# The first pair of b in two transfers of four rows (8 KB packets) in place of one of eight rows (16 KB packets)

## Chip, cores, metric

One core of one Trainium2 chip. The metric is the device time of one execution in microseconds. The profile's span, from the first to the last instruction, is some 1.8 us shorter than that time.

## The reference

```python
batch, m, k, n = 16, 512, 512, 512
a: (batch, k, m) float32      b: (batch, n, k) float32
out = np.matmul(a.transpose(0, 2, 1), b.transpose(0, 2, 1)).astype(np.float32)
```

The product sums over k. a lies with k first and is used as it comes; b lies with n first, and this kernel turns it on the chip. 33.6 MB are read and 16.8 MB written.

## The kernel before

Two batches of b form a pair. One transfer loads a pair into one of three buffers. VectorE casts it to bf16 in two halves, PE turns it, VectorE copies it out of PSUM. The SyncE queue (SP in the profile) issues all loads and the last stores; the ScalarE queue issues the other stores.

```python
b_v = b.rearrange("(p g) (ni r) k -> p (g ni) r k", g=2, r=NR)   # NR = 8 rows of 2 KB: 16 KB a partition
LOADS = 4; PAIRS = 3; OUTS = 5; LAG = 3; TAIL = 3
...
def run_sp(sp):
    for i in range(B):
        for p in ([0] if i == 0 else [(i + 1) // 2] if i % 2 and i + 1 < B else []):
            if p >= PAIRS:
                sp.wait_ge(turned, p - PAIRS + 1)
            sp.dma_start(b_sb[p % PAIRS][:], b_v[p]).then_inc(b_in[p % PAIRS], 16)
        s, use = i % LOADS, i // LOADS
        if use:
            sp.wait_ge(summed, MO * (i - LOADS) + 1)
        ...
        sp.dma_start(a_sb[s][:], a_v[i]).then_inc(a_in[s], 16)
...
def cast_b(p, h):                      # on VectorE, h = 0 and 1
    n = 3 if h and p + 1 == H else 1
    r = slice(h * NR // 2, (h + 1) * NR // 2)
    dve.wait_ge(b_in[p % PAIRS], 16 * (p // PAIRS + 1))
    dve.tensor_copy(b_bf[:, r, :], b_sb[p % PAIRS][:, r, :]).then_inc(bc_go, n)
```

Of the kernel before, what the change touches and what calls it, by code (L numbers as in the profile page):

```python
# [11 lines left out]
def kernel(  # L12
# [13 lines left out]
    NR = 2 * N // P  # L26
# [9 lines left out]
    b_v = b.rearrange("(p g) (ni r) k -> p (g ni) r k", g=2, r=NR)  # L36
# [3 lines left out]
    PAIRS = 3  # L40
# [10 lines left out]
    with tc.tile_critical():  # L51
# [4 lines left out]
        b_sb = [sb(f"b_sb{s}", [P, NR, K], f32) for s in range(PAIRS)]  # L56
# [12 lines left out]
        b_in = [sem(f"b_in{s}") for s in range(PAIRS)]  # L69
# [13 lines left out]
        def store(eng, j, part=slice(0, 2)):  # L83


            eng.dma_start(
                out_v[2 * j + part.start:2 * j + part.stop].rearrange("b p mo n -> p b mo n"),
                o_sb[j % OUTS][:, part],
            ).then_inc(o_out[j % OUTS] if j + OUTS < H else stored, 16)

        def run_sp(sp):
            for i in range(B):

                for p in ([0] if i == 0 else [(i + 1) // 2] if i % 2 and i + 1 < B else []):
                    if p >= PAIRS:
                        sp.wait_ge(turned, p - PAIRS + 1)
                    sp.dma_start(b_sb[p % PAIRS][:], b_v[p]).then_inc(b_in[p % PAIRS], 16)
                s, use = i % LOADS, i // LOADS
                if use:
                    sp.wait_ge(summed, MO * (i - LOADS) + 1)  # L100
                if i % 2 == 0 and i // 2 >= OUTS:

                    sp.wait_ge(o_out[i // 2 % OUTS], 16 * (i // 2 // OUTS))
                sp.dma_start(a_sb[s][:], a_v[i]).then_inc(a_in[s], 16)

            for j in range(H - TAIL, H - 1):
                sp.wait_ge(summed, MO * (2 * j + 2) + 3)
                store(sp, j)

            sp.wait_ge(summed, MO * (B - 1) + 1)  # L110
            sp.wait_ge(half_go, 1)
            store(sp, H - 1, slice(0, 1))
            sp.wait_ge(last_go, 3)
            store(sp, H - 1, slice(1, 2))
            sp.reg_mov(all_stored, 16 * STORED)
# [21 lines left out]
        def copy_out(eng, i, rm, go):  # L137

            q = rm if isinstance(rm, int) else rm.stop - 1
            eng.wait_ge(summed, MO * i + q + 1)  # L140
            copy = eng.copy if eng is nc.scalar else eng.tensor_copy
            h = q // 2
            p = rm - 2 * h if isinstance(rm, int) else slice(None)
            copy(o_sb[i // 2 % OUTS][:, i % 2, rm, :], o_ps[h][:, p, :]).then_inc(go, 1)  # L144

        def run_dve(dve):
            def cast_b(p, h):

                n = 3 if h and p + 1 == H else 1
                r = slice(h * NR // 2, (h + 1) * NR // 2)  # L150
                dve.wait_ge(b_in[p % PAIRS], 16 * (p // PAIRS + 1))
                dve.tensor_copy(b_bf[:, r, :], b_sb[p % PAIRS][:, r, :]).then_inc(bc_go, n)  # L152

            def turn(p, g):




                if g == 0:
                    dve.wait_ge(turned, p + 1)  # L160
                dve.tensor_copy(  # L161
                    bt_sb[g][:].rearrange("p j (ni r) -> p j ni r", r=NR),
                    bt_ps[:].rearrange("p j r (g ni) -> p g j ni r", g=2)[:, g],
                ).then_inc(bt_go, 1)

            cast_b(0, 0)
            cast_b(0, 1)
            turn(0, 0)
            for p in range(H):
                if p + 1 < H:  # L170
                    cast_b(p + 1, 0)
                copy_out(dve, 2 * p, slice(0, 2), od_go)
                turn(p, 1)
                if p + 1 < H:
                    cast_b(p + 1, 1)
                    copy_out(dve, 2 * p + 1, slice(0, 2), od_go)
                    turn(p + 1, 0)
            copy_out(dve, B - 1, slice(0, 2), last_go)
# [13 lines left out]
        def run_pe(pe):  # L192
# [41 lines left out]
            with pe.Fori(0, H) as _i:  # L234
# [6 lines left out]
                half(1, 1)  # L241

        run_sp(nc.sync)
        run_pool(nc.gpsimd)
        run_dve(nc.vector)
# [35 lines left out]
```

## Time and profile before

| | before |
|---|---|
| time, median of 6 runs | 124.83 us (124.61 to 125.09) |
| span of the profiled run | 123.0 us |
| PE / VectorE / ScalarE busy | 70% / 46% / 38% |
| 16 DMA engines busy, of the span | 97.3% (77.2 + 20.1) |
| packets, bytes | 5648, 50.33 MB, 409 GB/s over the span |

The last two rows decide how this kernel is read. The DMA engines are the busy ones, and they are busy from their first packet to their last (100.1% of the stretch from 1.9 to 121.5 us), so the time is made of a start, a block of packets and an end. The rows of the page that show it stand in the prediction.

### The profile page before, as it was taken

Reading aid. Unit: us, or ns where it says so; the run is one execution under the profiler, and the core shown is the slowest. Engines: PE = TensorE matmul, PEld = TensorE weight load, DVE = VectorE, ACT = ScalarE, POOL = GpSimd, SP = SyncE. Lnnn points to the kernel's source line nnn. Section 1 sums busy time; section 2 is a strip of 40 time slices with the busy share of each in tenths; the row PEclk is TensorE's granted clock in tenths of the full one; section 3 lists DMA queues with packets and bytes.
Section 4 is the critical chain, followed back from the end, with each engine's and each line's share of the span. In section 5 each row is a group of like instructions: output and inputs, shape, how many; then the busy total and the mean of one; then the engine's idle time right before and its main releaser. Section 6 shows DMA issues by size and latency. Waiting matters only on the chain. (4 is left out here: it accounts for less than half of the span.)

```text
span 123.0 us, 1086 instructions
## 1 busy us (share of the span) xinstructions
PE 86.1 (70%) x400; PEld 49.7 (40%) x400; DVE 56.4 (46%) x48; ACT 46.8 (38%) x34; POOL 0.7 (1%) x6
## 2 busy tenths in 40 slices
PE   0006497997999799779930799965992679979600
PEld 0006344642755464346410546442640526437300
DVE  0016368478295755917039107780719306171200
ACT  4003209537717903176300950329230490750300
POOL 2000000000000000000000000000000000000000
PEclk9999999999999999999995557999999558999995
DMA  4999999999999999999999999999999999999992
GB/s 91 394 400 458 400 424 456 429 394 456 426 397 448 434 376 432 426 440 440 416 421 429 458 408 418 429 426 437 453 397 432 426 426 426 429 426 426 429 424 115
DMA packets 5648, 50.33 MB, mean 409 GB/s; under 512 B 528, under 2 KB 528, under 8 KB 528
## 3 DMA queue, kind: packets, MB, share of 16 engines
q1 hardware_dynamic: 4288, 39.85, 77.2%
q10 hardware_dynamic: 1360, 10.49, 20.1%
HBM read 33.55 MB, written 16.78 MB: 409 GB/s over the span
## 5 line engine op out<-in xcount | busy, mean ns | idle before, releaser
L219 PE MATMUL o_ps<-bt_sb,a_bf 128*128 128x512 bf16 x256 | 65.1, 403 | 7.1 <-PEq L194 6.6
L135 ACT CAST a_bf<-a_sb 128x2048 bf16<-128x2048 f32 x16 | 30.4, 1900 | 40.8 <-DMA a_sb<-in_a_dram 40.8
L219 PEld LDWEIGHTS o_ps<-bt_sb,a_bf 128*128 128x128 bf16 x256 | 28.5, 115 | 37.5 <-issue 15.0
L205 PE MATMUL bt_ps<-identity,b_bf 128*128 128x128 f32 x144 | 24.3, 323 | 22.7 <-PEq L194 22.7
L144 DVE COPY o_sb<-o_ps 128x1024 f32<-128x1024 f32 x16 | 19.6, 1224 | 35.8 <-PE o_ps L219 35.8
L205 PEld LDWEIGHTS bt_ps<-identity,b_bf 128*128 128x128 f32 x144 | 22.2, 212 | 28.2 <-issue 27.2
L152 DVE CAST b_bf<-b_sb 128x2048 bf16<-128x2048 f32 x16 | 19.5, 1221 | 19.1 <-DMA b_sb<-in_b_dram 19.1
L144 ACT COPY o_sb<-o_ps 128x1024 f32<-128x1024 f32 (+1 forms) x17 | 16.4, 962 | 28.0 <-PE o_ps L219 28.0
L161 DVE COPY bt_sb<-bt_ps 128x1024 f32<-128x1024 f32 x16 | 19.5, 1216 | 3.1 <-PE bt_ps L205 3.1
L135 ACT ACT_TABLE_LOAD x1 | 1.3, 1283 | 0.9 <-SPq L51 0.9
L122 POOL TENSOR_SCALAR_AFFINE_SELECT identity<-identity 128x128 f32<-128x128 f32 x1 | 0.3, 294 | 0.2 <-POOL identity L120 0.2
L120 POOL MEMSET identity<- 128x128 f32 x1 | 0.2, 205 | 0.7 <-SPq L51 0.7
L265 POOL MEMSET const-bfloat16-1.0<- 128x1 bf16 x1 | 0.1, 102 | 0.0
L265 POOL MEMSET const-uint8-127<- 128x1 uint8 x1 | 0.1, 102 | 0.0
L265 POOL MEMSET const-float32-0.0<- 128x1 f32 x1 | 0.1, 99 | 0.2 <-issue 0.2
L265 POOL MEMSET const-float32-1.0<- 128x1 f32 x1 | 0.1, 99 | 0.0
## 6 DMA issues: line engine op xcount, KB each, us to landing
b_sb<-in_b_dram SPq DMA_DIRECT2D x8, 2048.0 KB, 20.4
a_sb<-in_a_dram SPq DMA_DIRECT2D x16, 1024.0 KB, 17.5
out_dram<-o_sb ACTq DMA_DIRECT2D x5, 2048.0 KB, 15.2
out_dram<-o_sb SPq DMA_DIRECT2D x2, 2048.0 KB, 13.6
out_dram<-o_sb SPq DMA_DIRECT2D x2, 1024.0 KB, 6.3
```

Source lines behind the costliest of these rows:

```text
L120: pool.memset(identity[:], 0.0).then_inc(id_go, 1)
L122: pool.affine_select(out=identity[:], in_=identity[:], compare_op=mybir.AluOpType.not_equal, fill=1.0, base=0, pattern=[[-1, P]], channel_ ...
L135: act.copy(a_bf[i % 2][:], a_sb[s][:]).then_inc(ac_go, 1)
L144: copy(o_sb[i // 2 % OUTS][:, i % 2, rm, :], o_ps[h][:, p, :]).then_inc(go, 1)
L152: dve.tensor_copy(b_bf[:, r, :], b_sb[p % PAIRS][:, r, :]).then_inc(bc_go, n)
L161: dve.tensor_copy(bt_sb[g][:].rearrange("p j (ni r) -> p j ni r", r=NR), bt_ps[:].rearrange("p j r (g ni) -> p g j ni r", g=2)[:, g],).the ...
L205: last = pe.transpose(bt_ps[:, j, r, :], w[:, r, j, :], identity[:])
L219: last = pe.matmul(o_ps[h][:, q, :], a_r[:, rk, 2 * h + q, :], bt_h[:, rk // 2, rk % 2, :], start=(rk == 0), stop=(rk == KO - 1),)
L265: nc = _bacc.Bacc("TRN2", target_bir_lowering=False, num_devices=1)
```

## The change

Its look is that of a split for an early start: load half of the first pair, cast it while the other half comes. But the wait that would use it is not there: both casts of pair 0 wait for both halves. What is left is a smaller packet and a second transfer, for the first pair alone.

```diff
-                    sp.dma_start(b_sb[p % PAIRS][:], b_v[p]).then_inc(b_in[p % PAIRS], 16)
+
+                    for r in (slice(0, NR // 2), slice(NR // 2, NR)) if p == 0 else (slice(0, NR),):
+                        sp.dma_start(
+                            b_sb[p % PAIRS][:, r, :], b_v[p][:, r, :]
+                        ).then_inc(b_in[p % PAIRS], 16)
...
-                dve.wait_ge(b_in[p % PAIRS], 16 * (p // PAIRS + 1))
+                dve.wait_ge(b_in[p % PAIRS], 16 * (p // PAIRS + 1 + (p % PAIRS == 0)))
```

## The prediction

> **What bounds the kernel now.** I first read the table of the page that cuts the span into 40 slices, because it says at once whether any engine is full from beginning to end.
>
> ```profile
> PE   0006497997999799779930799965992679979600
> DVE  0016368478295755917039107780719306171200
> ACT  4003209537717903176300950329230490750300
> ...
> DMA  4999999999999999999999999999999999999992
> GB/s 91 394 400 458 400 424 456 429 394 456 426 397 448 434 376 432 426 440 440 416 421 429 458 408 418 429 426 437 453 397 432 426 426 426 429 426 426 429 424 115
> ```
>
> No compute engine is full; the DMA row reads 9 in all slices but the first and the last. So the 16 DMA engines never run dry, and the span (123.0 us) is a start, a solid block of transfers, and an end. The page's chain of work that ended last holds 5% of the span in PE and stops at 110 us, so it does not describe the body. To measure the block I asked the DMA view for the stretch from 1.9 to 121.5 us alone:
>
> ```profile
> DMA packets 5648, 50.33 MB, mean 421 GB/s; under 512 B 528, under 2 KB 528, under 8 KB 528
> q1 hardware_dynamic: 4288, 39.85, 79.4%
> q10 hardware_dynamic: 1360, 10.49, 20.7%
> ```
>
> The shares are busy time over 16 engines: 79.4 + 20.7 = 100.1% of 119.6 us. Every packet of the program lies in it and there is no gap. The packet records of the trace have the first data packet at 1.956 us and the last one ending at 121.45 us, and the sum of all packet times after the start divided by 16 is 119.76 us (slightly above the 119.49 us between them, since one packet's end overlaps the next one's start). Hence span = 1.96 (start) + 119.5 (packets) + 1.5 (end of the last packet to the end of the program), and the metric is 1.8 us above the span (124.81 against 123.0). Only three things can move it: when the first packet starts, how long the packets take in total, and whether something opens a gap.
>
> Is the end also set by transfers? The timeline of the last stretch shows compute ending early:
>
> ```profile
> 115.02 0.59 ACT L144 COPY o_sb<-o_ps 128x512 f32<-128x512 f32 x1 [4.74 <-PE o_ps L219]
> 115.93 0.59 ACT L144 COPY o_sb<-o_ps 128x512 f32<-128x512 f32 x1 [0.32 <-PE o_ps L219]
> ```
>
> The last store is issued at 116.54 us and lands at 121.93 us. It is 1 MB, which is 2.47 us of packets (8 an engine at 309 ns), so they began near 119.0 us, behind stores still queued. Some 1.5 us of compute slack remains even at the end. At the start, the timeline has
>
> ```profile
> 0.95 0.39 SPq L97 DMA_DIRECT2D b_sb<-in_b_dram  x1
> ...
> 8.81 2.36 DVE L152 CAST b_bf<-b_sb 128x2048 bf16<-128x2048 f32 x2 [8.81 <-DMA b_sb<-in_b_dram]
> ```
>
> Issue at 0.95, first packet 1.0 us later, first use at 8.81, when the last of the 16 engines has reported (8.79 us in the records). While the compute engines wait for this, the DMA engines already move a0.
>
> [...] the median 16 KB packet takes 611 ns, 16384 / 611 = 26.8 GB/s an engine, 429 GB/s on 16. [...] the median 8 KB packet takes 309 ns, so two take 618 ns against 611 ns for one of 16 KB, 7 ns for one more packet. [...] each of the new halves is exactly 1 MiB over 128 partitions, and the a loads of this case are such transfers already. [...]
>
> **The change, part by part.**
>
> *Packets.* Pair 0 of b is 2 MB: now 128 packets of 16 KB, 8 an engine. Afterwards 256 of 8 KB, 16 an engine. Cost: 16 x 309 - 8 x 611 = 4944 - 4888 = +56 ns an engine. All engines are full, so this lies wholly on the path.
>
> *Completion.* One more transfer means 16 more semaphore packets, one an engine, 9 ns each in the records: +9 ns on the path. The 5648 packets become 5648 + 128 + 16 = 5792.
>
> *Issue.* One more issue on the SP queue, which takes 0.39 to 0.47 us with its gap to the next. The first half is issued at 0.95 us as before, so the first packet does not move. Everything behind it is issued some 0.45 us later, but finds a queue with microseconds of work: by the time a0 is issued (1.39, then about 1.85 us) no packet has moved at all, and a0's first packets follow some 5 us of b0. The last of the seven opening loads (a3) goes out at 4.23 us and lands at 28.5 us. The next refill waits on summed until 16.66 us, far later. Cost 0.
>
> *Waits.* The kernel's text decides this, not the transfer: for slot 0 both casts wait for one count of 16 more, that is 32 for pair 0, and both halves must have landed before either cast. So no cast starts on the first half early. The first cast starts when the second half has landed, about 8.81 + 0.065 = 8.87 us. For pairs 3 and 6 the offset only makes up for the extra 16 already counted. The listing of instructions by engine confirms that nothing else moves: PE, DVE, ACT and POOL keep their order, and SP has one transfer more.
>
> *Start-up.* The first packets are slow: 22 packets before 4 us take 0.65 to 1.92 us instead of 0.61; their excess over 611 ns is 12.5 us together, or 0.78 us an engine. If this is a wait that comes once, whatever the packet's size, it stays; if it goes with the bytes of the first packet, half of it could go. I take no change.
>
> Sum: +0.056 + 0.009 = +0.07 us, 124.81 -> 124.88 us, called 124.9.
>
> **The rivals.**
>
> *A quicker start.* Were the 0.78 us of slow first packets tied to their size, 8 KB packets might save up to about half, 0.4 us, giving 124.5. For it: the first packet of an engine is the slow one and is now twice as short. Against it: second packets in the records are slow as well (1.2 us), and then all become 611 ns at about the same moment, 3.5 to 4 us, which looks like a delay in time rather than in bytes. I give it one chance in four.
>
> *Half rows read more slowly.* Each half reads 8 KB, skips 8 KB, and so on, instead of running through memory. [...] Against: the b packets of 16 KB and the a packets of 8 KB already run at practically the same rate (429 and 424 GB/s)[...]. No view shows a read with this skip, so a few per cent of chance stay.
>
> *An earlier cast.* If the first cast could start on the first half, it would come some 2.5 us sooner (8 x 309 ns). The wait excludes it, and even then the compute engines would only wait longer later, since the DMA row has no gap to close. Worth 0.
>
> *A gap in the queue.* The phases of stores and loads might shift. The records show packets slowed to as much as 1.1 us at 42 to 48 us, where stores begin to mix with loads; they add up to 0.17 us an engine. A shift may change that by 0.1 us either way.
>
> **Range and chances.** The three times before run from 124.61 to 125.06, so a median of three may be off by 0.2 us. With 0.1 us for phases and the start-up chance of -0.4 us, 124.5 to 125.3 should hold 8 times in 10. Two per cent is 2.5 us. Nothing that this change touches can give 2.5 us back (the start-up excess is 0.78 us whole), and only the rival of the half rows could cost as much: faster 0.01, same 0.97, slower 0.02.
>
> **What would show it.** The changed profile should have 5792 packets, 50.33 MB, and the DMA row at 9 from slice 2 to 39; 1024 - 128 = 896 packets of 16 KB; 8 KB packets of pair 0 at 309 ns after the first few microseconds; the first cast at 8.8 to 9.0 us, not at 6; the span within 0.4 us of 123.0. A first cast below 8.6 us with fewer slow packets would speak for the quicker start; pair 0's packets well above 309 ns after 4 us for the half rows; a slice below 9 in the middle of the DMA row for a gap. Any of the last two of more than 0.4 us would make the prediction wrong.

The +0.07 us is made of measured packet times (611, 309 and 9 ns).

## More of the kernel before

One more view is needed for what follows: three stretches of the span, with the columns of the engines (busy time and number of instructions for PE, PE's weight loads, VectorE, ScalarE, GpSimd), then PE's clock, the busy share of the DMA engines, and GB/s. This is the kernel before:

```profile
1.00:9.00 8.00, 0.00 (x0) 0.00 (x0) 0.19 (x1) 1.19 (x1) 0.50 (x2) 1.00 0.86 325
40.00:50.00 10.00, 9.05 (x47) 5.30 (x46) 6.45 (x6) 4.11 (x4) 0.00 (x0) 1.00 0.99 413
50.00:100.00 50.00, 35.97 (x160) 20.23 (x159) 23.80 (x21) 20.05 (x15) 0.00 (x0) 0.85 1.01 429
```

The busy share is full in the second row (0.99) although less is moved than in the third (413 against 429 GB/s). A packet that is held up counts as busy in these records: in that row packets of 16 KB took up to 1.13 us in place of their median of 0.611, and no engine was without one. So where packets stalled here, the GB/s show it and the busy share does not. At 40 to 50 us the first store is issued (40.47 us) and its packets start to mix with the loads (from 44.04 us).

## The result, and the profile after

125.21 us, median of 6 runs (124.75 to 125.28), against 124.83 us. The ratio is 1.0023, 95% interval 1.0002 to 1.0043: within 2%, and inside the predicted range. A ratio is the mean time of one kernel's fast runs over that of the other's fast runs in the same rounds, so it is not quite the ratio of the medians.

The page of the changed kernel has the DMA rows and the packet count that the prediction named:

```profile
DMA  3999999999999989999999999999999999999992
GB/s 77 390 430 446 419 425 441 435 406 443 435 401 433 441 329 427 425 446 435 427 412 427 446 422 417 427 427 454 417 422 427 425 427 430 427 425 427 427 425 85
DMA packets 5792, 50.33 MB, mean 408 GB/s; under 512 B 544, under 2 KB 544, under 8 KB 544
```

The count of 5792 is exactly as predicted. The DMA row is not quite: it was to read 9 from slice 2 to slice 39, and the fifteenth slice (43 to 46 us) reads 8, with 329 GB/s where the row of before has 376. The prediction had named such a digit as the sign of a gap. By the packet records there is hardly one: between 6 us and the last 4 us of transfers each engine is without a packet for 0.03 us on the mean. It is slow packets that fill the slice. The timeline of the start, SP's issues and the first cast (columns: start, length, engine, line, operation, tiles, and what ended the idle time before):

```profile
0.95 0.86 SPq L99 DMA_DIRECT2D b_sb<-in_b_dram  x2
1.86 0.42 SPq L108 DMA_DIRECT2D a_sb<-in_a_dram  x1
...
8.67 2.36 DVE L156 CAST b_bf<-b_sb 128x2048 bf16<-128x2048 f32 x2 [8.67 <-DMA b_sb<-in_b_dram]
```

The second issue costs 0.47 us of the queue's time. The first cast comes at 8.67 us, not at 6, and a little before the 8.8 to 9.0 us of the prediction. The three stretches of the changed kernel, to be held against those of before:

```profile
1.00:9.00 8.00, 0.00 (x0) 0.00 (x0) 0.33 (x1) 1.19 (x1) 0.50 (x2) 1.00 0.88 334
40.00:50.00 10.00, 8.99 (x46) 5.29 (x46) 6.54 (x6) 4.00 (x4) 0.00 (x0) 1.00 0.99 402
50.00:100.00 50.00, 35.12 (x154) 19.99 (x156) 23.67 (x21) 19.65 (x14) 0.00 (x0) 0.85 1.01 429
```

At the start the changed kernel is ahead: 9 GB/s over 8 us is 0.07 MB, or 0.17 us at 429 GB/s. At 40 to 50 us it loses 11 GB/s over 10 us, 0.11 MB, 0.26 us. From 50 us on both run at the same rate. So two traces put the small loss at the place where stores begin. Is that the change, or chance?

To compare many traces I used the packet records in one way throughout. The *start excess* is the sum of what the packets up to 10 us took beyond 611 ns (16 KB) or 309 ns (8 KB), divided by 16 engines. The *store stall* is the same sum over the nine microseconds after the issue of the first store. The *engine idle* is the stretch from the first packet's start to the last packet's end, less the mean work of an engine (the sum of all packet times, each less the 3.5 ns by which consecutive packets of an engine overlap in the records, divided by 16). It holds the idle time of both ends of the stream: counted from the packets under way at each moment, the trace before has 0.33 us an engine before 6 us, where the engines begin one after another, and 0.57 us in the last 4 us, where they end one after another.

### The profile page after: what moved, and what is told of

Read it like the earlier page. It is cut to its first block, busy times and chain, and to the rows that moved or that the text cites. A ratio compares the mean times of both kernels' runs of the same rounds, so it can differ in the third digit from the quotient of the medians.

```text
span 123.4 us, 1079 instructions
## 1 busy us (share of the span) xinstructions
PE 85.5 (69%) x392; PEld 49.7 (40%) x400; DVE 56.5 (46%) x48; ACT 46.9 (38%) x34; POOL 0.7 (1%) x6
## 2 busy tenths in 40 slices
DMA packets 5792, 50.33 MB, mean 408 GB/s; under 512 B 544, under 2 KB 544, under 8 KB 544
## 5 line engine op out<-in xcount | busy, mean ns | idle before, releaser
L223 PE MATMUL o_ps<-bt_sb,a_bf 128*128 128x512 bf16 x248 | 63.1, 402 | 8.4 <-PEq L198 7.4
```

What stands on the lines that cost most here:

```text
L223: last = pe.matmul(o_ps[h][:, q, :], a_r[:, rk, 2 * h + q, :], bt_h[:, rk // 2, rk % 2, :], start=(rk == 0), stop=(rk == KO - 1),)
```

## The experiments

Twelve runs, each of five rounds against the kernel before; all results correct.

| run | median us | ratio (95% interval) |
|---|---|---|
| aa_before | 124.90 | 1.0009 (0.9993 to 1.0024) |
| aa_after | 125.17 | 1.0026 (1.0009 to 1.0043) |
| aa_after2 | 125.06 | 1.0017 (1.0000 to 1.0034) |
| split_all | 125.51 | 1.0058 (1.0043 to 1.0073) |
| pad_all | 125.66 | 1.0068 (1.0053 to 1.0084) |
| parts_first | 129.61 | 1.0377 (1.0361 to 1.0394) |
| pad_first | 125.18 | 1.0019 (1.0005 to 1.0032) |
| split_mid | 124.97 | 1.0010 (0.9992 to 1.0028) |
| early_cast | 124.98 | 1.0005 (0.9992 to 1.0018) |
| early_cast_2 | 125.19 | 1.0025 (1.0008 to 1.0041) |
| late_start | 125.76 | 1.0064 (1.0046 to 1.0082) |
| quarter_first | 125.37 | 1.0042 (1.0018 to 1.0066) |

**Is it real? aa_before, aa_after, aa_after2.** No edit: the two kernels again, against the kernel before.

> The kernel before against itself. The change measured +0.3 us (ratio 1.0023, interval 1.0002 to 1.0043). If that is real, this pair must give a ratio within 0.001 of 1. If two runs of one text differ by 0.002 or more, +0.3 us is within what chance gives. Trace: packets slowed at 40 to 50 us (where stores begin) cost 0.19 us an engine in the trace before and 0.49 us in the trace after; theory 'chance' has this number vary from run to run of one kernel, theory 'split' has it at 0.19 again.

> The changed kernel once more. Theory 'accounting plus chance' (7 ns for each further packet and 9 ns for the semaphore packet, +0.07 us in all, the rest of +0.3 us is the size of the stall where stores begin): ratio 1.0005, anything from 0.999 to 1.0025. Theory 'split' (the split start shifts the phase so that the stall is larger every time): ratio 1.002 to 1.003 again, and a stall of about 0.49 us an engine at 40 to 50 us in the trace.

> The changed kernel a third time, beside early_cast_2 on the same chip. 'Real' says 1.002 to 1.003 as twice before, landings spread by 0.8 us before 40 us and a stall over 0.3 us; 'chance' says anything from 0.999 to 1.0025 and a stall that may be as small as 0.1 us.

The kernel before against itself gives 1.0009; the changed kernel 1.0023, 1.0026 and 1.0017, every lower bound at 1.0000 or above. So the change costs something, some 0.2% or 0.27 us, about four times the 0.07 us of the accounting. A single ratio of 1.001 means nothing here, as the control shows. The store stall was 0.07 us in aa_before, 0.32 in aa_after and 0.45 in aa_after2. "Chance", as I had put it, falls for the stall. The landings' spread (how far apart the 16 engines report one load just before 40 us, without the first and the last of them) was 0.53 us in aa_after2 and not 0.8: that half of the expectation missed.

**Eight doses: split_all.**

```diff
-                    for r in (slice(0, NR // 2), slice(NR // 2, NR)) if p == 0 else (slice(0, NR),):
+                    for r in (slice(0, NR // 2), slice(NR // 2, NR)):
-  16 * (p // PAIRS + 1 + (p % PAIRS == 0))
+  32 * (p // PAIRS + 1)
```

> All eight pairs of b in two halves, eight times the dose. Accounting: 8 x (8 x 7 + 9) = 0.52 us, ratio 1.004, 6800 packets (5648 + 8 x 144). If each split costs the 0.3 us that was measured for one: +2.4 us, ratio 1.019. If the +0.3 us comes only from the start, or from chance: 1.004 to 1.006.

+0.72 us (0.0058 x 124.8), 6800 packets. A split pair does not cost 0.27 us each time: eight would be over 2 us. The rest of the chain, seven more split pairs, adds 0.45 us to the one split of the changed kernel, 0.06 us a pair.

**Small packets without a second transfer: pad_all and pad_first.** The two halves of a partition's row get a gap of 64 bytes between them in SBUF, for all pairs or for the first one only.

```diff
-        b_sb = [sb(f"b_sb{s}", [P, NR, K], f32) for s in range(PAIRS)]
+        b_sb = [sb(f"b_sb{s}", [P, 2, NR // 2 * K + 16], f32) for s in range(PAIRS)]
-                    sp.dma_start(b_sb[p % PAIRS][:], b_v[p]).then_inc(b_in[p % PAIRS], 16)
+                    sp.dma_start(b_sb[p % PAIRS][:, :, :NR // 2 * K],
+                                 b_v[p].rearrange("p (h r) k -> p h (r k)", h=2)).then_inc(b_in[p % PAIRS], 16)
...                                   # the casts read the same places; pad_first: the gap for p == 0 only
```

> All eight pairs in one transfer each, but the two halves of a row lie 64 bytes apart in SBUF, so every packet is 8 KB: packet size without a second transfer. Accounting: 8 x 8 x 7 ns = 0.45 us, ratio 1.0036, 5648 + 1024 = 6672 packets, none of 16 KB. If the second issue and landing is what costs, and not the packets: 1.000.

> The first pair in one transfer whose packets are 8 KB (a gap of 64 bytes between the halves of a row in SBUF), the other pairs as before. Accounting: 8 more packets an engine of 3.5 to 7 ns, 0.03 to 0.06 us, ratio 1.0004. If 8 KB packets at the start are what costs +0.3 us: 1.0025, with a larger stall at 40 to 50 us than the 0.07 and 0.18 us an engine of the two traces of the kernel before.

+0.85 us and +0.24 us. This would have been taken for "the packets alone do it", had the timeline not been read. Kernel pad_first:

```profile
0.95 0.65 SPq L104 DMA_DIRECT2D b_sb<-in_b_dram  x1
...
9.35 1.23 DVE L161 CAST b_bf<-b_sb 128x2048 bf16<-128x2048 f32 x1 [9.35 <-DMA b_sb<-in_b_dram]
```

The issue of the transfer with two pieces a partition takes 0.65 us instead of 0.39, and its first packet starts at 2.38 us instead of 1.96. That is a delay of 0.42 us of its own, so these two kernels do not isolate the packet size. What pad_first does tell: its store stall is 0.14 us, as with the kernel before, though pair 0 came in the same 8 KB packets. The page of pad_first counts 5776 packets, the 128 more that this takes. The expectation that 8 KB packets at the start enlarge that stall failed, in one trace and with a later start.

**A second transfer without small packets: parts_first.**

```diff
-                    for r in (slice(0, NR // 2), slice(NR // 2, NR)) if p == 0 else (slice(0, NR),):
+                    for r in (slice(0, P // 2), slice(P // 2, P)) if p == 0 else (slice(0, P),):
-                            b_sb[p % PAIRS][:, r, :], b_v[p][:, r, :]
+                            b_sb[p % PAIRS][r], b_v[p][r]
```

> The first pair in two transfers as in the change, but each of 64 partitions with packets of 16 KB: a second issue and landing without smaller packets. Accounting: one more semaphore packet, under 10 ns, ratio 1.000. If the second transfer at the start is what costs +0.3 us (twice measured, 1.0023 and 1.0026): 1.0025.

+4.7 us, which neither theory had. The DMA view of this kernel, 3.5 to 7.5 us, while pair 0 comes:

```profile
DMA packets 68, 0.85 MB, mean 213 GB/s; under 512 B 16, under 2 KB 16, under 8 KB 16
q1 hardware_dynamic: 68, 0.85, 101.6%
```

All engines busy, half the rate: a 16 KB packet takes 1.28 us (median from 4.3 to 7 us) in place of 0.611. That is 213 GB/s where 16 KB in 0.611 us on each of 16 engines make 429. Why was not shown: no other run changes the partitions of a transfer. As a control this kernel is spoilt. It does show, once more, what a delay at the start is worth: the first cast slips from 8.81 to 13.30 us, by 4.49 us, and the time grows by about as much (4.7 us).

**The same split elsewhere: split_mid.**

```diff
-  if p == 0 else (slice(0, NR),):
+  if p == 4 else (slice(0, NR),):
-  16 * (p // PAIRS + 1 + (p % PAIRS == 0))
+  16 * (p // PAIRS + 1 + (p in (4, 7)))
```

> The split on pair 4 (issued near 55 us) and not on pair 0: the same packets and transfers in number, but the start and the place where stores begin as before. If the change costs by what it does to the start and to the stall at 40 to 50 us: 1.000 to 1.0005, stall 0.07 to 0.18 us. If a split pair costs 0.3 us wherever it stands: 1.0025.

1.0010, no different from the control (1.0009), with the same 5792 packets. The intervals overlap that of the changed kernel, so the time alone does not separate them; the stall does, 0.21 us in the one trace. But the expectation had placed pair 4 wrongly. SP's timeline of split_mid:

```profile
27.60 0.91 SPq L99 DMA_DIRECT2D b_sb<-in_b_dram  x2
```

Pair 4 is issued at 27.60 us, not near 55 (that is pair 6), and its packets pass just where stores begin: all 312 data packets of loads in the nine microseconds after the first store's issue are of 8 KB, where the kernel before has 105 of 16 KB and 103 of 8 KB. So split_mid keeps the start as before, but not that place. It shows that a split pair passing there is not enough for the large stall; it does not show what a split in an undisturbed stretch costs. Split_mid, 40 to 50 us, and below it aa_after2, the changed kernel:

```profile
40.00:50.00 10.00, 8.98 (x47) 5.25 (x46) 6.54 (x6) 4.10 (x4) 0.00 (x0) 1.00 1.01 419
```

```profile
40.00:50.00 10.00, 9.00 (x46) 5.51 (x48) 6.53 (x7) 3.85 (x4) 0.00 (x0) 1.00 1.00 406
```

**The wait that the change left in place: early_cast, early_cast_2.** The first half gets a semaphore of its own, so that its cast need not wait for the second.

```diff
+        b_first = sem("b_first")
-  ).then_inc(b_in[p % PAIRS], 16)
+  ).then_inc(b_first if p == 0 and r.start == 0 else b_in[p % PAIRS], 16)
-  dve.wait_ge(b_in[p % PAIRS], 16 * (p // PAIRS + 1 + (p % PAIRS == 0)))
+  if p == 0 and h == 0:
+      dve.wait_ge(b_first, 16)
+  else:
+      dve.wait_ge(b_in[p % PAIRS], 16 * (p // PAIRS + 1))
```

> The change with a semaphore of its own for the first half, so that the first cast no longer waits for the second half. First cast at 6.2 us (the last engine's landing of the first half in the trace after is 6.17) and not 8.67. If the kernel is bound by its transfers, the time stays that of the changed kernel, ratio 1.0015 to 1.003 against the kernel before. If the wait for both halves was what kept the change from paying, up to 2.4 us come back: 0.981 to 0.99.

> The early first cast again. Its ratio was 1.0005 (0.9992 to 1.0018) where the changed kernel had 1.0023 and 1.0026, though both move the same packets. If the early cast gives something back, it must again be 0.001 to 0.002 below aa_after2; if that was chance, both agree within 0.001.

The timeline of early_cast on VectorE:

```profile
6.18 1.23 DVE L160 CAST b_bf<-b_sb 128x2048 bf16<-128x2048 f32 x1 [6.18 <-DMA b_sb<-in_b_dram]
8.66 1.23 DVE L160 CAST b_bf<-b_sb 128x2048 bf16<-128x2048 f32 x1 [1.26 <-DMA b_sb<-in_b_dram]
```

The cast starts 2.5 us earlier, and the time is 1.0005 and 1.0025, around that of the changed kernel. The difference that the first run seemed to show was gone in the second (1.0025 beside 1.0017). Starting compute earlier bought nothing here, where the transfers have no gap.

**The start itself: late_start.** The kernel before, its first issue held until the identity is built.

```diff
         def run_sp(sp):
+            sp.wait_ge(id_go, 2)
```

> The kernel before, with the first transfer issued only when the identity is ready (last POOL instruction ends at 1.83 us), so near 1.9 us in place of 0.95 us. If span = start + full block of packets + end, the whole 0.9 to 1.0 us shows: ratio 1.0075. If slack anywhere takes it up (compute waiting for b, buffers): nearer 1.000. It also tells how the two padded kernels read, whose first packet came 0.42 us later.

The first packet starts at 2.88 us (1.96 before), 0.92 us later; the time grows by 0.80 us (0.0064 x 124.98; interval 0.57 to 1.02). The start is on the path, nearly or fully one for one. At that rate the 0.42 us of the padded kernels would cost some 0.37 us (an estimate, 0.42 x 0.80 / 0.92). All of pad_first cost 0.24 us (0.06 to 0.40), so how much of its delay reached the time is not settled.

**The change's dose at the start: quarter_first.**

```diff
-  for r in (slice(0, NR // 2), slice(NR // 2, NR)) if p == 0 else (slice(0, NR),):
+  for r in [slice(x, x + 2) for x in range(0, NR, 2)] if p == 0 else [slice(0, NR)]:
-  16 * (p // PAIRS + 1 + (p % PAIRS == 0))
+  16 * (p // PAIRS + 1 + 3 * (p % PAIRS == 0))
```

> The change's own dose: pair 0 in four transfers of two rows, 4 KB packets. Accounting by spacing: 24 more packets an engine and three more semaphore packets, 3.5 and 5.5 ns each, 0.10 us, ratio 1.0008. If smaller packets at the start leave the 16 engines further apart and the stall where stores begin grows with it (spread of a load's landings just before 40 us, without first and last: 0.5 us before, 0.8 us after; stall 0.07 to 0.18 and 0.33 to 0.58 us): 1.0025 or more with stall over 0.3 us.

1.0042, 0.52 us, more than the change itself and five times the accounting. But not through the stall: the landings lay 0.92 us apart and the store stall was only 0.09 us. So the idea that the spread of the engines sets the stall falls. Its loss is at the start. The first of the three stretches, which in the kernel before has 325 GB/s:

```profile
1.00:9.00 8.00, 0.00 (x0) 0.00 (x0) 0.00 (x0) 1.19 (x1) 0.50 (x2) 1.00 0.84 298
```

27 GB/s less over 8 us are 0.22 MB, or 0.50 us at 429 GB/s: the whole loss. The engine idle is 1.44 us (0.97 to 1.05 in the kernel before), and 0.59 us of it lies before 6 us (0.14 to 0.33 in the four traces of the first table below); at the end it is 0.75 us (0.57 to 0.79 there). With four small transfers the engines stood without a packet for longer at first; why was not tested.

**The traces side by side** (us, defined above). Pair 0 in one 16 KB transfer, all engines on all partitions:

| trace | start excess | store stall | engine idle |
|---|---|---|---|
| before | 0.80 | 0.18 | 0.97 |
| aa_before | 1.01 | 0.07 | 1.05 |
| split_mid | 0.85 | 0.21 | 0.96 |
| late_start | 1.04 | 0.09 | 0.98 |
| mean | 0.93 | 0.14 | 0.99 |

Pair 0 in two transfers of 8 KB packets, the other pairs as before (the changed kernel, and the same with the early cast):

| trace | start excess | store stall | engine idle |
|---|---|---|---|
| after | 0.71 | 0.49 | 1.17 |
| aa_after | 0.84 | 0.32 | 1.29 |
| aa_after2 | 0.70 | 0.45 | 0.89 |
| early_cast | 0.73 | 0.58 | 0.97 |
| early_cast_2 | 0.53 | 0.51 | 1.16 |
| mean | 0.70 | 0.47 | 1.10 |

The other five:

| trace | start excess | store stall | engine idle |
|---|---|---|---|
| split_all | 0.72 | 0.18 | 1.42 |
| pad_all | 0.99 | 0.14 | 1.01 |
| pad_first | 0.84 | 0.14 | 1.28 |
| quarter_first | 0.98 | 0.09 | 1.44 |
| parts_first | 4.18 | 0.03 | 0.93 |

The stall columns of the first two tables do not overlap; the start columns overlap a little (0.80 in the trace before, 0.84 in aa_after), and those of the engine idle wholly, so its difference is not shown to be more than chance. The difference of the means is -0.23 + 0.33 + 0.11 = +0.21 us, with 0.03 us for the packets 0.24 us; the three ratios of the changed kernel average 1.0022, 0.27 us.

The stall is a matter of loads alone. In the trace after, its slow packets are all of loads (of 16 KB, up to 1.19 us in place of 0.611); no packet of a store in those nine microseconds took over 0.32 us. Load packets that had started before the first store packet (43.94 us, 3.57 us after the store's issue) hold 0.29 of the 0.49 us.

No version beat the kernel before.

## Why the prediction was right, and where it was not

*The block of transfers bounds the kernel.* Shown: a later first packet costs nearly its whole delay (late_start, 0.80 us for 0.92), a cast 2.5 us earlier nothing (early_cast, twice). The changed kernel's DMA row stays full but for the one digit 8. Not shown is the prediction's 1.5 us of slack at the end: it allows 1.0 us from the last store's issue to its first packet, as for a load, but the first store's packets came 3.57 us after its issue (40.47 and 44.04 us).

*Packets and completion, +0.065 us.* The duration was right: 309 ns is the median of the 207 packets of 8 KB that start from 4 to 8 us in the trace after. The sum was too large. I had seen that packet ends overlap the next starts and did not carry it into the step. By spacing a 16 KB packet holds its engine for 607.5 ns and two of 8 KB for 611, so the term is 8 x 3.5 + 5.5 = 33 ns, not 65.

*Issue, 0.* Right: the first packet starts at 1.96 us in both, and nothing behind waited (0.03 us without a packet between 6 us and the last 4 us). The first issue was as short as before (0.39 us); in pad_first it took 0.65 us, and the first packet came 0.42 us later.

*Waits: no early cast.* Right, and shown not to matter. The moment was not: 8.87 us was forecast, and three traces of the changed kernel have 8.67, 9.06 and 8.62 us, so the start itself varies by more than the 0.065 us that was added.

*Half rows read more slowly.* Refuted by the same 207 packets: their median of 309 ns is that of all 8 KB packets of the kernel before.

*Start-up, "I take no change".* The rival with one chance in four was half right: with pair 0 in two transfers the slow start is shorter, 0.70 instead of 0.93 us an engine over nine traces (0.72 in split_all). That the packet size does it is not shown: with 8 KB packets in one transfer it was 0.84 and 0.99 us (pad_first, pad_all), with 4 KB packets 0.98 (quarter_first). It is not half of the 0.78 us, and it is given back.

*"A shift may change that by 0.1 us either way."* This is the step that failed: the stall where stores begin grew by 0.33 us on the mean, in five of five traces. The largest term was one that I had called noise. The sum had no term for the engine idle either, about 1 us; here its change is not clear of chance, but in quarter_first it is some 0.4 us.

That the result lies in the range is partly luck: a shorter start (-0.23 us) and a longer stall (+0.33 us), neither of them in the sum, nearly cancel. The mechanism was right in that the DMA engines bound the kernel and the early cast is worth nothing; the size, 0.07 for 0.27 us, was not.

*Open.* Why the stall is larger after a halved first pair. One trace each speaks against the packet size of pair 0 (pad_first, stall 0.14 us, but with a later start), against the mere number of packets (split_mid, 0.21) and against the spread of the engines (quarter_first, spread 0.92 us and stall 0.09). Split_all has the same start and a stall of 0.18 us, but its other pairs are 8 KB too. It is a regular effect of the changed kernel, with or without the early cast, and no cause is shown.

## What to carry to other kernels

Where the DMA row is full from end to end, do not look for the worth of a split in the first compute instruction: here 2.5 us earlier bought nothing (1.0005 and 1.0025, the changed kernel 1.0017 to 1.0026). Ask what the split does to the start of the stream (quarter_first lost its 0.5 us there) and to the place where stores begin. Read GB/s beside the busy share, since a stalled packet counts as busy (in the changed kernel at 40 to 50 us 402 GB/s at a share of 0.99, from 50 us on 429 at 1.01). And below half a per cent measure the kernel against itself first, and repeat: one run of early_cast said 1.0005, the next 1.0025.
